# Queries and keys of the last four mLSTM heads as a thirteenth block of the seven-product stage

## The chip, the core and the metric

The kernel runs on one core of one Trainium2 chip. The core has five engines that run side by side, each through its own list of instructions and in order: TensorE (PE in the profile) multiplies matrices into PSUM, VectorE (DVE) and ScalarE (ACT) work element by element, GpSimd (POOL) does the rest of the elementwise work, and SyncE (SP) issues most of the transfers. ACT and POOL issue transfers too. All transfers share sixteen DMA engines. The metric is the device time of one execution in microseconds (us).

## The reference

One decoder layer over 512 tokens of width 2048, in float32. A normalised input is projected by one wide matrix, two token mixers run on parts of the projection, and their outputs are projected back, gated and added.

```
u    = rmsnorm(x, norm_w);  proj = u @ w_in          # 512 x 2048 by 2048 x 20528
ml_q, ml_k (8 heads x 128 each), ml_v, ml_o, ml_z (2048 each), ml_i, ml_f (8 each),
dn_qkv (3 x 2048), dn_z (2048), dn_b, dn_a (16 each), gate_a, gate_b (2048 each) = split(proj)

h_a = mlstm_chunkwise(q * 128**-0.5, k, v, softcap(ml_i + b_i), logsigmoid(softcap(ml_f + b_f)))
h_a = rmsnorm_per_head(h_a) * ml_norm_w * sigmoid(ml_o) * silu(ml_z)
q, k, v = silu(causal_conv4(dn_qkv));  q, k = l2norm(q), l2norm(k)
h_b = gated_delta_chunkwise(q, k, v, sigmoid(dn_b), -exp(a_log) * softplus(dn_a + dt_bias))
h_b = rmsnorm_per_head(h_b, dn_norm_w) * silu(dn_z)
h   = x + sigmoid(gate_a) * (h_a @ w_out[:2048]) + sigmoid(gate_b) * (h_b @ w_out[2048:])
out = rmsnorm(h, final_norm_w)
```

Here only `ml_q` and `ml_k` of heads 4 to 7 matter: 512 columns of `w_in` each, so a product of 512 x 2048 by 2048 x 1024. The mLSTM needs them channel-major (128 channels of a head by 512 tokens, `kq`), and the keys token-major too (`kw`).

## The kernel before

**Products.** Each float32 operand is split into a rounded high part and the rest (`split_hi` on ACT, L135, and `split_lo` on DVE, L138), and each product is three matmuls: high by high, high by low, low by high.

**Two ways to project.** `proj_cm` (L250) gives 256 columns channel-major: two PSUM tiles of 128 channels by 512 tokens, with the weights as the stationary operand; 96 matmuls on lines L261 to L263. `seven` (L565, within `seven_stage`) gives a block of twice 512 columns, `c1` and `c2`, token-major, by a Strassen-like scheme: seven products in place of eight, over 16 sets of weights a block (8 of group A with four products, 8 of group B with three), each product six matmuls on L578 to L580. Sums and differences of weights are made on DVE (L531, L532, L538); one of them goes to DRAM (`t_d`) in group A and is read back in group B. The weights are prepared one set ahead of the products. A "sink" for each kind of block takes the four results: two row tiles come straight from PSUM when a product ends (`end1`, `end5`), two more lie in the SBUF tiles U1 and C22 (`end7`) until the next block writes these. `sink_s` (L697, the DN_Z gates) does for each of eight tiles a copy, a tanh, one vector operation (L704) and a store.

**The order of the work.** PE's instructions run in the order in which the program writes them. The other work is written as generators that a scheduler of the kernel's own advances: `start(gen, wait)` puts one in, and `tick()` advances all that are due. `proj_cm` ticks 16 times in a projection (once for six matmuls), `seven` once for each product (six matmuls too). The other engines' instructions are ordered by a list scheduler with priorities; `urgent` raises one, `behind(e)` holds an instruction until after the newest split or weight load of that engine.

**The stages.** (1) Norms, u, and four projections (`QK`, L145) with queries and keys of heads 0 to 3, stored to `qk_d`. (2) Twelve `seven` blocks (`SEVEN`, L49): four z, two s, two v, four g. (3) The mixers: eight units (`dn_unit`, L1058; `UNITS`, L47), each with projections of K, V and Q of two delta heads (three times 16 ticks). In units 3 to 6 a projection of kind "m" between K and V gives queries and keys of mLSTM head 4, 5, 6 or 7 (128 columns of each), which ACT copies from PSUM to `mkq` (L1076, L1078). (4) The output: two plain blocks, in which unit 7's mixers end, then one more plain block, two seven-product blocks and a last plain one. A tile pool of three PSUM banks, `psw`, serves all small products of the mixers.

**The mixers' chains.** After a unit's projections `dn_back` (L946) starts 25 ticks later, or 9 where the unit had an "m" projection; 11 ticks after that two chains, `dn_chain` (L999), go over four token blocks, handing small products from PE to DVE and ACT and back. `ml_head` (L1099) takes one mLSTM head: it turns the keys token-major (`turn`, L807: a transpose on DVE in 32 x 32 blocks, then `travel`, L814: four stores of 64 KB to DRAM and a load), makes the decay weights, then goes over four token blocks with `pnum` (L1142, L1144) and `pcs`. Heads 0 to 3 come in through `ml_first` (L1184), which loads `kq` from `qk_d`; they start 40 ticks apart. Heads 4 to 7 start behind their own projection. The buffers `mkq`, `mkw` and `mv1` exist once.

```
for h in range(2 * QKFIRST):
    start(ml_first(h), 1 + 40 * h, "B")
for unit in UNITS:
    dn_unit(*unit)
```

Of the kernel before, what the change touches and what calls it, by code (L numbers as in the profile page):

```python
# [15 lines left out]
P = 128  # L16
# [39 lines left out]
def hybrid_body(  # L56
# [83 lines left out]
    def behind(eng):  # L140

        return tc.issue_after(newest[eng])
# [5 lines left out]
    for p, h in UNITS:  # L148
        for kind, c in (("i", DN_K + p * NB), ("m", h), ("i", DN_V + p * NB), ("i", DN_Q + p * NB)):
            if c is not None:  # L150
                plan += [(kind, c, k) for k in range(0, KT, KP)]
# [7 lines left out]

    def load_raw():  # L160
        kind, c, k = plan[len(raws)]
        if kind == "m":

            qk = w_in[k * P:(k + KP) * P, ML_Q:ML_V].rearrange("(k p) (a n) -> p k a n", p=P, a=2)[:, :, :, c * P:(c + 1) * P]
            src, nk, n = None, KP, NB
        elif kind == "i":
            src, nk, n = w_in[k * P:(k + KP) * P, c:c + NB], KP, NB
        else:
            src, nk, n = w_out[k * P:(k + 1) * P, c:c + NO], 1, NO
        with tc.high_priority(offset=2 * PRIO if len(raws) > RAHEAD else 0):  # L170
            raw = wp.tile([P, nk, n], F32, tag="wr", name="wr", bufs=NRAW)
            if src is None:
                for i in range(KP):
                    nc.sync.dma_start(raw[:, i, :].rearrange("p (a n) -> p a n", a=2), qk[:, i])
            else:
                newest["S"] = nc.sync.dma_start(raw, src.rearrange("(k p) n -> p k n", p=P)).ins
        raws.append((raw, nk, n))

    def split_next():
# [67 lines left out]

    JB, WB, OB = (psj, "pj"), (psw, "wk"), (pso, "o")

    def proj_cm(col0, before=None, kind="i"):  # L250
        ps = [psj.tile([P, S], F32, tag="pj", name="pj") for _ in range(2)]
        for kt0 in range(0, KT, KP):
            hi, lo = next_w(kind, col0, kt0)
            if before is not None:
                for k in range(KP):
                    before(kt0 + k)
            for j in range(2):
                for k in range(KP):
                    kt = kt0 + k
                    wsl = slice(j * P, (j + 1) * P)  # L260
                    T.matmul(ps[j], hi[:, k, wsl], uh[:, kt, :], start=(kt == 0), stop=False)  # L261
                    T.matmul(ps[j], hi[:, k, wsl], ul[:, kt, :], start=False, stop=False)  # L262
# [368 lines left out]
    def sink_flat(dst, func, scale):  # L631

        def sink(c1, c2, m1, m5, m7, last):
            def out_(ps, c, col):
                o = spare(last)
                with urgent(3):
                    A.activation(o, ps, func, scale=scale)
                nc.scalar.dma_start(dst(c, col), o)

            def late(x_, c, col):  # L640
                with behind("A"):
                    if func != AF.Copy:
# [12 lines left out]

            return (lambda t: out_(m1[t], t, c1)), end5, end7
        return sink
# [39 lines left out]
    def sink_s(c1, c2, m1, m5, m7, last):  # L697
# [21 lines left out]
        def end7(t):  # L719
# [3 lines left out]

        return (lambda t: out_(m1[t], t, c1, 4)), end5, end7

    SINK = {"g": sink_flat(lambda c, col: tg_d[c, :, col - GATE:col - GATE + NO], AF.Tanh, 0.5),
            "v": sink_flat(lambda c, col: v_d[c, :, col - ML_V:col - ML_V + NO], AF.Copy, 1.0),
            "z": sink_z, "s": sink_s}

# [269 lines left out]
    def dn_chain(j, hs, kq, u):  # L999
# [53 lines left out]
        yield 2  # L1053
        with urgent():
            V.tensor_tensor(out=g, in0=po, in1=g, op=ALU.mult)
        turn(g, h_d[h], True, 5 if h < 2 * UNITS[-1][0] else 3)

    def dn_unit(p, mh):  # L1058
        hs = (2 * p, 2 * p + 1)
        dcol = p * NB  # L1060
        even, last = p % 2 == 0, p == UNITS[-1][0]
        by, front = "B" if even else "A", "B" if even or last else "A"
        u = {"aq": [], "qt": [], "ke": [], "vs": [], "dm": [], "pool": wkb if even else wk}
        kq = [u["pool"].tile([P, 2, S], F32, tag="kq", name=f"kq{h}", bufs=2) for h in hs]
# [4 lines left out]
            conv_silu(ps[j], 16 + hs[j], kq[j][:, 0, :])  # L1069
            start(silu_end(kq[j][:, 0, :], (kq[j][:, 0, :], ke)), 4 + 3 * j, front)  # L1070
        start(dn_front_k(hs, kq, u), 1, front)
        if mh is not None:
            ps = proj_cm(mh, kind="m")
            mkq = wkb.tile([P, 2, S], F32, tag="mkq", name="mkq", bufs=1)
            with urgent():
                A.mul(mkq[:, 1, :], ps[0], float(P) ** -0.5)  # L1076
            with urgent():
                A.copy(mkq[:, 0, :], ps[1])  # L1078
            start(ml_head(mh, mkq), 1, "B")
        ps = proj_cm(DN_V + dcol)  # L1080
        for j in range(2):
            vt = u["pool"].tile([P, NC, P], F32, tag="vn", name="vt", bufs=2)
# [11 lines left out]
            u["qn"].append(qn)  # L1094
            start(silu_end(kq[j][:, 1, :], (kq[j][:, 1, :], qn)), 4 + 3 * j, front)
        start(dn_front_q(hs, kq, u), QWAIT + 3 * last, by)
        start(dn_back(hs, kq, u), (25 if mh is None else 9) + 4 * last, by)

    def ml_head(h, kq):  # L1099
        kT, qT = kq[:, 0, :], kq[:, 1, :]  # L1100
        kw = wkb.tile([P, NC, P], F32, tag="mkw", name="kw", bufs=1)
        with behind("V"):
            turn(kT, kw)
        rb = row_bcast(h, "nrb")
        iwb = wp.tile([P, NC, P], F32, tag="tg", name="iwb", bufs=3)
        G.dma_start(iwb.rearrange("p c t -> p (c t)"), rows_d[8 + h, :].partition_broadcast(P))
# [74 lines left out]
            turn(g[i], hm_d[2 * h + i], True)  # L1181
            yield 4

    def ml_first(h):  # L1184

        kq = wkb.tile([P, 2, S], F32, tag="mkq", name="mkq", bufs=1)
        for i in range(2):
            nc.sync.dma_start(kq[:, 1 - i, :], qk_d[2 * QKFIRST * i + h])
        yield 4
        yield from ml_head(h, kq)  # L1190

    y_d = dr.tile([NC, P, D], F32, tag="yd", name="y_d")

    def open_y():
# [37 lines left out]
            if i > 3:  # L1232
                yield 1

    for h in range(2 * QKFIRST):
        start(ml_first(h), 1 + 40 * h, "B")
    start(open_y(), 200)
    for unit in UNITS:
        dn_unit(*unit)

    h1s, h2s = ctx.enter_context(ExitStack()), ctx.enter_context(ExitStack())
    late = {}
# [446 lines left out]
```

## Time and profile before

| | |
|---|---|
| median of 3 runs | 2215.1 us (2213.11 to 2217.27) |
| profiled execution | 2216.45 us, its span 2214.7 us |
| mean granted TensorE clock | 0.995 |
| PE busy | 97% |
| DVE, ACT, POOL busy | 75%, 46%, 13% |

An "L" number is a line of the kernel. In a row of a group the columns are line, engine, operation, output and inputs, shapes and count, then busy time, mean of one, idle time before. In a row of one line or tile they are the shortest, median and longest duration in ns and the first and last start. In a row of waits: who waited for whom, total us, how often, the longest. In a row of DMA issues: output and input, queue, count, size and the median time from issue to landing. Matmuls overlap, so their durations exceed the step from one to the next.

### The profile page before, as it was taken

What the parts mean: (1) busy time and instruction counts of PE and PEld (TensorE: products, weight loads), DVE (VectorE), ACT (ScalarE), POOL (GpSimd) and SP (SyncE); (2) the same over time, 40 slices, a digit from 0 to 9 for tenths busy, and PEclk for the clock granted to TensorE, in tenths of its full rate; (3) what the DMA queues carried; (4) which work ended last, traced back from release to release, by engine and by line L of the source; (5) the groups of instructions that cost most, each with busy time, mean ns of one, the idle gap of its engine ahead of it and who ended that gap; (6) DMA issues with size and microseconds to landing.
All of it is one profiled execution on the core that took longest, in us unless ns stands there. A gap on an engine that the chain in (4) does not pass through costs nothing. (4 is left out here: it accounts for less than half of the span.)

```text
span 2214.7 us, 31661 instructions
## 1 busy us (share of the span) xinstructions
PE 2153.5 (97%) x10592; PEld 1767.6 (80%) x10592; DVE 1664.4 (75%) x2891; ACT 1024.1 (46%) x1986; POOL 290.7 (13%) x395
## 2 busy tenths in 40 slices
PE   6999999999999999999999999999999999989998
PEld 5877878878888878878888887878888887867776
DVE  5787788788878777777588876757685877577777
ACT  5444444445444444443545644444444454344345
POOL 0320000000000000000223314222222211010100
PEclk9999999999999999999999999999999999999999
DMA  5455666667667766776677767677757668696896
GB/s 157 119 182 188 199 211 195 214 190 239 198 214 233 230 184 224 235 220 219 186 191 177 181 157 179 144 172 171 183 141 173 152 160 231 175 263 187 244 301 215
DMA packets 531174, 433.72 MB, mean 196 GB/s; under 512 B 241857, under 2 KB 393634, under 8 KB 530882
## 3 DMA queue, kind: packets, MB, share of 16 engines
q1 hardware_dynamic: 418738, 345.09, 55.0%
q10 hardware_dynamic: 105568, 68.77, 9.8%
q0 software_dynamic: 6704, 17.83, 3.8%
q8 instruction: 83, 1.36, 0.3%
q14 instruction: 81, 0.66, 0.1%
HBM read 342.37 MB, written 93.39 MB: 197 GB/s over the span
## 5 line engine op out<-in xcount | busy, mean ns | idle before, releaser
L135 ACT CAST wh<-wr 128x512 fp32r<-128x512 f32 (+1 forms) x538 | 379.5, 707 | 417.8 <-PE pj L262 230.3
L138 DVE TENSOR_TENSOR wl<-wr,wh 128x512 fp32r<-128x512 f32 (+1 forms) x538 | 443.0, 826 | 148.0 <-ACT wh L135 134.8
L261 PE MATMUL pj<-uh,wh 128*128 128x512 f32 x1024 | 426.5, 416 | 0.0
L263 PE MATMUL pj<-uh,wl 128*128 128x512 f32 x1024 | 400.9, 391 | 0.0
L262 PE MATMUL pj<-ul,wh 128*128 128x512 f32 x1024 | 400.4, 391 | 0.0
L579 PE MATMUL ps<-wl,uh 128*128 128x512 f32 x704 | 278.1, 395 | 8.1 <-DVE wl L138 7.8
L578 PE MATMUL ps<-wh,uh 128*128 128x512 f32 x704 | 275.7, 392 | 6.5 <-DVE X L626 4.0
L580 PE MATMUL ps<-wh,ul 128*128 128x512 f32 x704 | 274.4, 390 | 0.0
L135 ACT CAST wh<-ts 128x512 fp32r<-128x512 f32 x224 | 138.3, 617 | 262.4 <-DVE ts L538 201.2
L135 ACT CAST wh<-t 128x1024 fp32r<-128x1024 f32 x112 | 117.9, 1053 | 250.1 <-PE ps L580 125.3
L263 PEld LDWEIGHTS pj<-uh,wl 128*128 128x128 f32 x1024 | 192.4, 188 | 42.4
L579 PE MATMUL ps<-wl,suh 128*128 128x512 f32 x576 | 224.2, 389 | 1.6 <-DVE wl L138 1.6
L578 PE MATMUL ps<-wh,suh 128*128 128x512 f32 x576 | 224.7, 390 | 0.9 <-ACT qk L353 0.5
L580 PE MATMUL ps<-wh,sul 128*128 128x512 f32 x576 | 224.1, 389 | 0.0
L261 PEld LDWEIGHTS pj<-uh,wh 128*128 128x128 f32 x1024 | 193.2, 189 | 35.0
L262 PEld LDWEIGHTS pj<-ul,wh 128*128 128x128 f32 x1024 | 193.4, 189 | 32.9
L138 DVE TENSOR_TENSOR wl<-ts,wh 128x512 fp32r<-128x512 f32 x224 | 153.4, 688 | 35.2 <-ACT wh L135 35.2
L138 DVE TENSOR_TENSOR wl<-t,wh 128x1024 fp32r<-128x1024 f32 x112 | 137.0, 1224 | 51.0 <-ACT wh L135 50.5
L579 PEld LDWEIGHTS ps<-wl,uh 128*128 128x128 f32 x704 | 132.1, 188 | 47.7 <-DVE wl L138 21.9
L578 PEld LDWEIGHTS ps<-wh,uh 128*128 128x128 f32 x704 | 132.1, 188 | 40.0 <-DVE X L626 9.6
L538 DVE TENSOR_TENSOR ts<-wr 128x512 f32<-128x512 f32 x112 | 77.2, 689 | 101.0 <-DMA wr<-t_d 80.1
L580 PEld LDWEIGHTS ps<-wh,ul 128*128 128x128 f32 x704 | 132.2, 188 | 26.2
(313 smaller groups left out, 3513.9 us busy)
## 6 DMA issues: line engine op xcount, KB each, us to landing
wr<-in_w_in_dram SPq DMA_DIRECT2D x704, 256.0 KB, 3.7
wr<-in_w_out_dram SPq DMA_DIRECT2D x138, 256.0 KB, 4.7
t_d<-ts ACTq DMA_DIRECT2D x96, 256.0 KB, 4.1
wr<-t_d SPq DMA_DIRECT2D x96, 256.0 KB, 4.0
wr<-in_w_in_dram SPq DMA_DIRECT2D x64, 128.0 KB, 3.2
xt<-in_x_dram SPq DMA_DIRECT2D x8, 512.0 KB, 7.6
tg_d<-X ACTq DMA_DIRECT2D x16, 256.0 KB, 5.5
tg_d<-to ACTq DMA_DIRECT2D x16, 256.0 KB, 5.1
```

What stands on the lines that cost most here:

```text
L135: newest["A"] = A.copy(hi, src).ins
L138: newest["V"] = V.tensor_tensor(out=lo, in0=src, in1=hi.bitcast(F32), op=ALU.subtract).ins
L261: T.matmul(ps[j], hi[:, k, wsl], uh[:, kt, :], start=(kt == 0), stop=False)
L262: T.matmul(ps[j], hi[:, k, wsl], ul[:, kt, :], start=False, stop=False)
L263: T.matmul(ps[j], lo[:, k, wsl], uh[:, kt, :], start=False, stop=(kt == KT - 1))
L538: V.tensor_tensor(out=ts[:, 0, :], in0=r[:, 0, :], in1=r[:, 2, :], op=ALU.subtract)
L578: T.matmul(ps[t], ah, hi, start=(g == "A" and i == 0), stop=False, skip_group_check=True)
L579: T.matmul(ps[t], ah, lo, start=False, stop=False, skip_group_check=True)
L580: T.matmul(ps[t], al, hi, start=False, stop=(i == KH - 1), skip_group_check=True)
```

## The change

`UNITS` loses its second part: no unit has an "m" projection any more, and each lasts 48 ticks. `SEVEN` gains a block "q" between s and v, whose `c1` is the queries and `c2` the keys of heads 4 to 7 (`QKS` is 512). Its `sink_q` scales the queries by 128 ** -0.5, stores the keys token-major to `k_d` and turns all eight tiles of 128 tokens by 512 columns: one transpose on DVE and four stores of 64 KB on ACT's queue into `qt_d`, which holds the heads channel-major. `ml_first` goes into `ml_head`: every head loads `kq` from DRAM, heads 0 to 3 from `qk_d` and 4 to 7 from `qt_d`. Heads 0 to 3 still turn their keys; heads 4 to 7 load `kw` from `k_d`. All eight heads start 42 ticks apart, and `dn_back` starts 25 ticks after each unit (29 after the last, as before).

```
-UNITS = [(p, p + 1 if 2 * QKFIRST - 2 < p < 7 else None) for p in range(8)]
+UNITS = list(range(8))
+QKS = 2 * QKFIRST * P
          + [("s", DN_Z + c, DN_Z + c + NO) for c in range(0, D, 2 * NO)]
+         + [("q", ML_Q + QKS, ML_K + QKS)]
          + [("v", ML_V + c, ML_V + c + NO) for c in range(0, D, 2 * NO)]
...
+    qt_d = dr.tile([4 * QKFIRST, P, S], F32, tag="qtd", name="qt_d")
+    k_d = dr.tile([NC, P, QKS], F32, tag="kd", name="k_d")
...
+    def sink_q(c1, c2, m1, m5, m7, last):
+
+        def turned(x_, c, a):
+            if a:
+                with behind("A"):
+                    nc.scalar.dma_start(k_d[c], x_)
+            o = spare(True)
+            with behind("V"):
+                V.transpose(o, x_)
+            to = qt_d[a * 4:(a + 1) * 4].rearrange("h (j r) (n a c) -> r (h j) n a c", r=BS, n=NC, c=BS)
+            ov = o.rearrange("p (m c) -> p m c", c=BS)
+            for b in range(4):
+                yield 1
+                with behind("A"):
+                    nc.scalar.dma_start(to[:, :, c, b, :], ov[b * BS:(b + 1) * BS])
+
+        def out_(ps, t, a, wait):
+            z = spare(False)
+            with urgent(3):
+                A.mul(z, ps, (float(P) ** -0.5, 1.0)[a])
+            start(turned(z, t, a), wait + 6 * t)
+
+        def end5(t):
+            add(m5[t], U1[t], m5[t])
+            out_(m5[t], t, 1, 8)
+
+        def late_q(t):
+            with behind("A"):
+                A.mul(U1[t], U1[t], float(P) ** -0.5)
+            yield from turned(U1[t], 2 + t, 0)
+
+        def end7(t):
+            add(U1[t], U1[t], m7[t])
+            start(turned(C22[t], 2 + t, 1), 14 + 6 * t)
+            start(late_q(t), 17 + 6 * t)
+
+        return (lambda t: out_(m1[t], t, 0, 4)), end5, end7
...
-        if mh is not None:
-            ps = proj_cm(mh, kind="m")
-            mkq = wkb.tile([P, 2, S], F32, tag="mkq", name="mkq", bufs=1)
-            with urgent():
-                A.mul(mkq[:, 1, :], ps[0], float(P) ** -0.5)
-            with urgent():
-                A.copy(mkq[:, 0, :], ps[1])
-            start(ml_head(mh, mkq), 1, "B")
...
-        start(dn_back(hs, kq, u), (25 if mh is None else 9) + 4 * last, by)
+        start(dn_back(hs, kq, u), 25 + 4 * last, by)
 
-    def ml_head(h, kq):
+    def ml_head(h):
+        kq = wkb.tile([P, 2, S], F32, tag="mkq", name="mkq", bufs=1)
+        kw = wkb.tile([P, NC, P], F32, tag="mkw", name="kw", bufs=1)
+        first = h < 2 * QKFIRST
+        for i in range(2):
+            nc.sync.dma_start(kq[:, 1 - i, :], (qk_d if first else qt_d)[2 * QKFIRST * i + h % (2 * QKFIRST)])
+        yield 4
         kT, qT = kq[:, 0, :], kq[:, 1, :]
-        kw = wkb.tile([P, NC, P], F32, tag="mkw", name="kw", bufs=1)
-        with behind("V"):
-            turn(kT, kw)
+        if first:
+            with behind("V"):
+                turn(kT, kw)
+        else:
+            with behind("S"):
+                nc.sync.dma_start(kw, k_d[:, :, h * P - QKS:(h + 1) * P - QKS].rearrange("c p n -> p c n"))
...
-    for h in range(2 * QKFIRST):
-        start(ml_first(h), 1 + 40 * h, "B")
+    for h in range(MLH):
+        start(ml_head(h), 1 + 42 * h, "B")
```

More of the change, by code (lines that the diff above doesn't have):

```diff
@@ L147, in hybrid_body @@
     nfront = len(plan)
[L148 to L151, printed above, removed]
+    for p in UNITS:
+        for c in (DN_K, DN_V, DN_Q):
+            plan += [("i", c + p * NB, k) for k in range(0, KT, KP)]
     plan += [("o", nb * NO, k) for nb in range(D // NO - 1) for k in range(KT)]
@@ L161, in load_raw @@
         kind, c, k = plan[len(raws)]
[L162 to L166, printed above, removed]
+        if kind == "i":
             src, nk, n = w_in[k * P:(k + KP) * P, c:c + NB], KP, NB
@@ L171, in load_raw @@
             raw = wp.tile([P, nk, n], F32, tag="wr", name="wr", bufs=NRAW)
[L172 to L176, printed above, removed]
+            newest["S"] = nc.sync.dma_start(raw, src.rearrange("(k p) n -> p k n", p=P)).ins
         raws.append((raw, nk, n))
@@ L248, in hybrid_body, with proj_cm @@
     JB, WB, OB = (psj, "pj"), (psw, "wk"), (pso, "o")
-    def proj_cm(col0, before=None, kind="i"):
+    def proj_cm(col0, before=None):
         ps = [psj.tile([P, S], F32, tag="pj", name="pj") for _ in range(2)]
         for kt0 in range(0, KT, KP):
-            hi, lo = next_w(kind, col0, kt0)
+            hi, lo = next_w("i", col0, kt0)
             if before is not None:
@@ L1055, in dn_chain, with dn_unit @@
             V.tensor_tensor(out=g, in0=po, in1=g, op=ALU.mult)
-        turn(g, h_d[h], True, 5 if h < 2 * UNITS[-1][0] else 3)
-    def dn_unit(p, mh):
+        turn(g, h_d[h], True, 5 if h < 2 * UNITS[-1] else 3)
+    def dn_unit(p):
         hs = (2 * p, 2 * p + 1)
         dcol = p * NB
-        even, last = p % 2 == 0, p == UNITS[-1][0]
+        even, last = p % 2 == 0, p == UNITS[-1]
         by, front = "B" if even else "A", "B" if even or last else "A"
@@ L1182, in ml_head @@
             yield 4
[L1184 to L1190, printed above, removed]
     y_d = dr.tile([NC, P, D], F32, tag="yd", name="y_d")
@@ L1233, in load_h @@
                 yield 1
-    for h in range(2 * QKFIRST):
-        start(ml_first(h), 1 + 40 * h, "B")
+    for h in range(MLH):
+        start(ml_head(h), 1 + 42 * h, "B")
     start(open_y(), 200)
     for unit in UNITS:
-        dn_unit(*unit)
+        dn_unit(unit)
     h1s, h2s = ctx.enter_context(ExitStack()), ctx.enter_context(ExitStack())
```

2 lines of the change are left out of this document (1 added, 1 removed).

## The prediction

> **What bounds the kernel now.** I read the engine table first, then the busy times by stage, then what TensorE waited for inside each stage. The stage borders are where the matmul stream changes its line.
>
> ```profile
> span 2214.7 us, 31661 instructions
> PE 2153.5 (97%) x10592; PEld 1767.6 (80%) x10592; DVE 1664.4 (75%) x2891; ACT 1024.1 (46%) x1986; POOL 290.7 (13%) x395
> L261 PE MATMUL pj<-uh,wh 128*128 128x512 f32 x1024 | 426.5, 416 | 0.0
> ...
> 206.80:1063.00 856.20, 848.72 (x3697) 690.13 (x3696) 678.28 (x858) 387.34 (x560) 1.44 (x9) 1.00 0.68 212
> 1063.00:1838.20 775.20, 769.21 (x4418) 643.49 (x4417) 564.39 (x1373) 386.48 (x1004) 213.16 (x288) 1.00 0.71 171
> ```
>
> The last two rows are stretches: borders and length, then busy time (and count) of PE, PEld, DVE, ACT and POOL, the granted clock, the DMA share and GB/s. The first holds blocks 2 to 12 of the seven-product stage, the second the 28 projections of the mixer stage. PE is idle for 7.5 us of 856.2 in the one and for 6.0 us of 775.2 in the other; DVE is busy 79% and 73%. Both stages are set by the number of matmuls that PE issues. A matmul's "mean ns of one" (416) is not its price, since matmuls overlap; the price is the step between starts:
>
> ```profile
> 1063.02 0.39 PE L261 MATMUL pj<-uh,wh 128*128 128x512 f32 x1
> ...
> 1076.85 0.39 PE L262 MATMUL pj<-ul,wh 128*128 128x512 f32 x1
> ```
>
> These are the first and the 62nd of an unbroken run at the start of the first K projection: 13.83 us over 61 steps, 0.2267 us each.
>
> **The change, part by part.**
>
> Removed: four projections of kind "m" (heads 4 to 7). The row above has L261 x1024 for 32 projections, so 32 matmuls on each of three lines, 96 in all. 96 x 0.2267 = 21.8 us each, **-87.1 us** of PE time in the mixer stage, all of it on the path, as PE has no idle time there to speak of.
>
> Added: a thirteenth block of the seven-product stage, 56 products of 6 matmuls = 336 where the four projections had 384. The eleven blocks of the first stretch last 856.2 / 11 = 77.8 us, their waits included: **+77.8 us**. Net -9.3 us. That is all of the gain: one matmul in eight of a 512 x 1024 projection.
>
> The new block's own load beside PE. Its preparation (sums, splits, the round trip of the stored sum) is every block's and is in the 77.8. Its sink does eight tiles: eight PSUM or SBUF tiles scaled or copied on ACT, eight 128x512 transposes on DVE, four plain stores and 32 stores of 64 KB on ACT's queue. The nearest sink is that of DN_Z, which does eight vector operations of the same size:
>
> ```profile
> 518.70:596.20 77.50, 77.00 (x337) 62.81 (x337) 63.92 (x83) 36.86 (x55) 0.00 (x0) 1.00 0.72 222
> L704 DVE SCALAR_TENSOR_TENSOR to<-to x8: 680/682/686, 517.3 to 604.5; 128x512 f32<-128x512 f32 x8
> L811 DVE STREAM_TRANSPOSE to<-vt x16: 691/704/712, 1118.2 to 1825.6; 128x512 f32<-128x512 f32 x16
> L821 ACTq DMA_DIRECT2D hm_d<-to x64: 309/310/1627, 1132.8 to 1786.3; - x64
> ```
>
> A transpose (0.704 us) costs DVE what that sink's operation (0.682 us) costs, so DVE stays at 63.9 of 77.5 us with PE idle for half a microsecond. ACT issues 36 DMAs in place of 8: 28 more x 0.31 = 8.7 us, on top of 36.9 of 77.5. What is queued behind them on ACT is the rounding of the next weights (L135), then DVE's subtraction (L138), then PE; a store that waits for its transpose holds all three. These run one set of weights ahead of PE, 3 to 4 products or 4.1 to 5.4 us (six matmuls are 1.36 us), and the four stores of a tile come one product apart. I take 0 for it; the bounds are -0.7 (no wait in it at all, 7.5 us over 11 blocks) and +3.4, the eight tiles at the mean wait of such a block, 4.4 us in 11:
>
> ```profile
> PE ps L579 <- DVE wl L138: 4.4, 11, 0.9
> ```
>
> That is 0.4 us per wait, 3.2 for eight, and I round it up. Were the cover of one set gone, each tile would show its 0.7 us.
>
> The 32 stores have 512 pieces of 128 bytes each, 16384 packets. Their like is in the mixer stage, 64 of them for hm_d alone:
>
> ```profile
> q10 hardware_dynamic: 105568, 68.77, 9.8%
> t_d<-ts ACTq DMA_DIRECT2D x96, 256.0 KB, 4.1
> hm_d<-to ACTq DMA_DIRECT2D x64, 64.0 KB, 3.6
> ```
>
> One lands in 3.6 us, a whole 256 KB store in 4.1. The queue's packets took 9.8% of 2214.7 us for 105568, 2.06 ns each of all sixteen engines; that mean holds the 2 KB packets too, so 16384 x 2.06 = 34 us is a ceiling. By bytes (2 MB of 68.77) it is 6.6 us, a floor. They spread over some 30 products (42 us), when the weights take a share of about 0.7. I take the lower half, because a 64 KB store lands no later than a large one; then the rings hold and nothing waits. The Trainium skill, "DMA: Bandwidth & Descriptors", Specifications, asks for at least 512 bytes per transfer and says that below it the engine reads, modifies and writes. Here the landing times do not show that penalty; with it the ceiling would hold, which is rival three.
>
> Mixer stage, the work that stays. SP loses 64 loads of 128 KB; for heads 4 to 7 it also loses the turn of k (20 DMAs) and gains three loads each, 12. DVE loses 32 subtractions and four transposes, ACT 32 roundings and eight copies out of PSUM:
>
> ```profile
> L138 DVE TENSOR_TENSOR wl<-wr,wh x538: 641/689/2655, 19.3 to 2180.1; 128x512 fp32r<-128x512 f32 x142, 128x1024 fp32r<-128x1024 f32 x38
> L1076 ACT ACTIVATE mkq<-pj x4: 597/598/600, 1367.2 to 1701.8; 128x512 f32<-128x512 f32 x4
> L1188 SPq DMA_DIRECT2D mkq<-qk_d x8: 326/423/1001, 1029.2 to 1257.3; - x8
> ```
>
> DVE: 564.4 - 32 x 0.689 - 4 x 0.70 = 539.5 us in 775.2 - 87.1 = 688.1, 78%: as dense as the seven-product stage, where PE hardly waits. The kq load of a head stands on SP ahead of weight loads and needs the previous head's mkq free, some 37 ticks after its start; heads were 40 ticks apart and are now 42, and no issue of that load lasted over 1.0 us. I take nothing for it.
>
> What gets denser can be seen in units that had no "m" block. Units 1, 2 (three projections), 3, 4, 5, 6 (four) and 7 (three):
>
> ```profile
> 1135.50:1220.00 84.50, 84.50 (x512) 70.76 (x510) 71.35 (x176) 44.19 (x111) 25.14 (x37) 1.00 0.78 188
> 1220.00:1308.20 88.20, 87.47 (x533) 73.09 (x532) 68.08 (x178) 47.76 (x131) 27.16 (x39) 1.00 0.76 180
> 1308.20:1427.00 118.80, 116.02 (x670) 96.87 (x670) 87.59 (x227) 56.59 (x162) 33.99 (x49) 1.00 0.64 148
> 1427.00:1538.40 111.40, 108.93 (x626) 90.91 (x625) 76.30 (x186) 52.98 (x139) 27.08 (x36) 1.00 0.75 177
> 1647.00:1755.50 108.50, 108.50 (x625) 90.92 (x624) 75.74 (x186) 51.75 (x136) 28.89 (x40) 1.00 0.65 155
> 1755.50:1838.20 82.70, 82.70 (x507) 69.38 (x506) 61.90 (x130) 45.23 (x117) 22.28 (x23) 1.00 0.69 174
> ```
>
> Unit 1 has DVE at 84% and PE idle for nothing; unit 2 waits 0.7 us. The dense shape is not what makes PE wait; the waits of 2.8 and 2.5 us stand in units 3 and 4. But one thing is new. Before, heads 4 to 7 had their C-chain at ticks 52 to 68 of a unit and the delta chains at 20 to 40. With a head every 42 ticks and a back half 25 ticks after each unit, the chain of head 5 (ticks 234 to 250) falls on the delta chains of unit 3 (228 to 248), head 6 on unit 4, head 7 on unit 5. Three streams then hand PSUM banks of one pool of three to DVE and ACT. Their waits in the mixer stage now:
>
> ```profile
> PE p L993 <- ACT s L989: 2.5, 1, 2.5
> PE pk L860 <- DVE kq L795: 2.2, 1, 2.2
> PE pw L1021 <- DVE r L1016: 1.1, 2, 0.7
> ```
>
> A hand-over waits 0.5 us in the mean of L1021. I take one for each of the four heads, **+2 us**; the bounds are -6.0 (every wait of the stage gone) and five units at unit 3's 2.8, less the 5.3 of units 3 and 4, +8.7.
>
> The end of the mixers: unit 6's delta chains shift 16 ticks towards the first output block, where one bank of their pool is taken. Unit 7's chains run there already, and that stretch (1838 to 1998 us) waits for these:
>
> ```profile
> PE py L1330 <- DVE gz L1055: 5.3, 1, 5.3
> PE py L1330 <- ACT wh L135: 2.5, 1, 2.5
> PE py L1330 <- ACT yp L779: 1.7, 2, 1.3
> PE py L1331 <- DVE wl L138: 0.7, 1, 0.7
> ```
>
> The longest is for the last gate (L1055), which unit 7 sets in both kernels; none is for a bank of that pool. The front of unit 7 ends about 22 ticks after its last projection, unit 6's chains now about 20, so buffers are given back no later. 0, with the same bounds as above.
>
> **The sum.** The profiled execution took 2216.45 us (span 2214.7), 1.35 above the median of 2215.1. 2216.45 - 87.1 + 77.8 + 2 = 2209.2; taken from the median, 2207.8. I say **2208**. From no change a measurement of this kernel tells about 0.2%, 4.4 us.
>
> **The rivals.**
>
> One: the waits grow to the bound of +8.7 and take the gain. 2215.1 - 9.3 + 8.7 = 2214.5. For it: units 3 and 4 did wait. Against: units 1 and 2.
>
> Two, the other side: the three streams on one pool open a wait of 2.5 us at each of the four heads, and the clock halves after it. The clock shows this after the last gate:
>
> ```profile
> 1945.00:1955.00 10.00, 7.31 (x24) 5.92 (x25) 7.30 (x13) 2.18 (x3) 0.88 (x1) 0.67 0.80 176
> 1974.00:1999.00 25.00, 21.81 (x84) 17.14 (x83) 18.39 (x27) 11.31 (x19) 4.87 (x7) 0.86 1.01 344
> ```
>
> 0.33 of 10 us is 3.3 us lost after the 5.3 us wait, and 0.14 of 25, 3.5 us, about one of 2.5 us. So 4 x (2.5 + 3.4) = 23.6, 2215.1 - 9.3 + 23.6 = 2229. It decides from 2.3 us per head on. Against it: unit 4's wait of 2.5 us left the clock at 1.00. The Trainium skill, "TensorE: Matmul & The Clock Gate", Part 1, has the clock halved after an idle window of about 3.4 us; by that rule waits of 2.5 us would cost only themselves, some 2216. The second row shows a halved clock with the shorter wait, so I keep the higher price.
>
> Three: the small stores take the ceiling of 34 us of the rings. 0.7 x 77.8 + 34 = 88 us of transfers in 77.8: the weights come 10 us late, 2216.
>
> Four: better than said. No wait in the new block and half of the mixers' 6.0 us gone: 2215.1 - 9.3 - 0.7 - 3.0 = 2202; with all gone 2199.
>
> **How the numbers follow.** My forecast 0.47 (2203.5 to 2211), rival one 0.19, three 0.05, two 0.16, four 0.13. The range leaves out most of rival two and the tail of four: 2199 to 2219; the forecast's own is 2203.5 to 2211. Faster by over 0.2% means under 2210.7: the forecast less a little and rival four, 0.58. Within: the rest of it, one and three, 0.26. Slower: rival two, 0.16.
>
> **What the profile after would show.** L261 to L263 x896 in place of 1024; t_d stores x104; the mixer stage near 690 us with DVE near 78%, thirteen blocks of about 77.8 us, the one behind the new block included. Wrong, if the block after it is over 81 us with waits for L138 (ACT held, or the rings), if units 3 to 7 last over 89 us each with waits at the C-chain or L1021, or if the granted clock falls below 1.00 within the mixers.

## The result and the profile after

Over 22 runs each, the changed kernel takes 2217.5 us and the kernel before 2213.1: a ratio of 1.002 (95% interval 1.0011 to 1.0029), slower by 4.3 us where 7 us less was forecast. Executions of one kernel spread over 12 to 14 us. The profiled execution of before lay 3.3 us above the median of its kernel (2216.45 us), that of after at its median (2217.26), so the two traces differ by 0.8 us only; the other 3.5 us can't be placed in them.

The same views as before: the engine table, the group of the first projection line, and stretches of the seven-product stage from its first block to its last and of the mixers' units 0 to 6 (columns as in the prediction).

```profile
span 2215.5 us, 31630 instructions
PE 2146.3 (97%) x10544; PEld 1762.6 (80%) x10544; DVE 1695.5 (77%) x2937; ACT 1035.8 (47%) x1994; POOL 293.8 (13%) x395
L256 PE MATMUL pj<-uh,wh 128*128 128x512 f32 x896 | 374.1, 417 | 0.7 <-ACT yp L812 0.7
...
125.60:1141.70 1016.10, 1003.85 (x4370) 817.51 (x4369) 806.92 (x1017) 457.80 (x659) 8.15 (x17) 1.00 0.68 212
1141.70:1748.80 607.10, 598.45 (x3504) 500.87 (x3502) 462.51 (x1183) 314.10 (x830) 191.66 (x257) 0.99 0.74 181
```

The saving is there. L256 (L261 before) went from x1024 to x896, and PE has 48 matmuls less, 10.9 us at the step of 0.2267. But PE's busy time fell by only 7.2 us (2153.5 to 2146.3), since part of the work ran at a halved clock, and its idle time grew from 61.2 to 69.2 us. The growth has four places. For three of them these are PE's waits: in the block behind the new one (672 to 754 us), in units 0 to 6 with most of unit 7 (1142 to 1829), and from unit 7 to the start of the output (1749 to 1850):

```profile
PE ps L574 <- DVE wl L142: 3.2, 2, 3.1
...
PE pk L893 <- DVE kq L828: 7.8, 4, 5.3
PE pj L256 <- ACT yp L812: 0.7, 1, 0.7
...
PE pst L1061 <- ACT w L1057: 1.5, 2, 1.1
PE pr L1046 <- DVE st L1067: 1.3, 1, 1.3
PE pw L1054 <- DVE r L1049: 0.4, 1, 0.4
```

The fourth is the output from 1850 to 2000 us, where PE is idle for 10.8 us in place of 8.5. The wait for the rounding of weights there (L1356 for L139) is 3.7 us in this trace and 5.3 us in a second one of the same kernel; no run was made for it, and it stays open.

And these are stretches: the block behind the new one, twelve microseconds in it, the block after that, then units 4 and 5 and twenty microseconds of unit 5.

```profile
672.00:754.10 82.10, 78.74 (x338) 64.01 (x337) 64.67 (x84) 33.27 (x47) 0.00 (x0) 0.98 0.78 215
700.00:712.00 12.00, 8.99 (x32) 7.29 (x33) 7.96 (x11) 4.49 (x7) 0.00 (x0) 0.86 0.95 256
754.10:830.20 76.10, 76.10 (x337) 63.05 (x336) 59.52 (x74) 32.74 (x46) 0.00 (x0) 1.00 0.70 219
...
1472.90:1562.40 89.50, 88.51 (x540) 74.34 (x538) 68.89 (x179) 47.05 (x131) 27.25 (x37) 1.00 0.74 181
1562.40:1660.10 97.70, 91.67 (x541) 76.88 (x540) 70.26 (x179) 47.75 (x130) 29.10 (x39) 0.97 0.69 169
1605.00:1625.00 20.00, 14.69 (x146) 12.05 (x145) 14.30 (x40) 11.27 (x31) 7.72 (x11) 0.83 0.89 214
```

A wait of 3.1 us for L142 and the halved clock behind it (0.14 of 12 us, 1.7 us lost) make that block 82.1 us where its neighbours take 76 to 78. A wait of 5.3 us for the keys of unit 5's second head, and again a halved clock (0.17 of 20, 3.4 us), make unit 5 97.7 us where unit 4 takes 89.5. The timeline of the first place shows how it comes about (ACT, then DVE; start, duration, line; in brackets the idle time before and what ended it):

```profile
691.56 3.78 ACTq L735 DMA_DIRECT2D qt_d<-to  x4
695.46 1.05 ACT L139 CAST wh<-t 128x1024 fp32r<-128x1024 f32 x1 [4.05 <-DMA qt_d<-to]
...
695.61 0.71 DVE L729 STREAM_TRANSPOSE to<-X 128x512 f32<-128x512 f32 x1 [1.36 <-DMA t_d<-ts]
...
701.67 0.71 DVE L729 STREAM_TRANSPOSE to<-X 128x512 f32<-128x512 f32 x1 [1.73 <-DMA t_d<-ts]
702.30 0.65 DVE L142 TENSOR_TENSOR wl<-ts,wh 128x512 fp32r<-128x512 f32 x1
```

ACT stood 4.05 us with four stores of turned data to issue, the rounding of the next weights behind them; DVE stood 1.4 and 1.7 us in front of a transpose, because its output shares three buffers with the sums of weights, whose store was still running; and the subtraction that PE waited for stood behind that transpose.

The second place, unit 5 (DVE, then PE):

```profile
1606.68 0.69 DVE L1214 TENSOR_TENSOR mg<-v,mg 128x512 f32<-128x512 f32 x1
...
1607.97 0.70 DVE L844 STREAM_TRANSPOSE to<-mg 128x512 f32<-128x512 f32 x1
...
1611.08 0.68 DVE L1157 TENSOR_TENSOR wm<-psc,wm 128x512 f32<-128x512 f32 x1
1611.68 0.68 DVE L828 SCALAR_TENSOR_TENSOR kq<-th,kq 128x512 f32<-128x512 f32 x1
...
1612.51 2.04 PE L893 MATMUL pk<-kq 128*128 128x128 f32 x8 [5.31 <-DVE kq L828]
```

Ahead of the keys (L828) DVE has the end of head 5, which is its output gates and their transposes (`mg`, L1214 and L844), and the first product of head 6 (`wm`, L1157).

### The profile page after: what moved, and what is told of

Read it like the earlier page. It is cut to its first block, busy times and chain, and to the rows that moved or that the text cites. A ratio compares the mean times of both kernels' runs of the same rounds, so it can differ in the third digit from the quotient of the medians.

```text
span 2215.5 us, 31630 instructions
## 1 busy us (share of the span) xinstructions
PE 2146.3 (97%) x10544; PEld 1762.6 (80%) x10544; DVE 1695.5 (77%) x2937; ACT 1035.8 (47%) x1994; POOL 293.8 (13%) x395
## 3 DMA queue, kind: packets, MB, share of 16 engines
q10 hardware_dynamic: 124192, 74.02, 10.8%
## 5 line engine op out<-in xcount | busy, mean ns | idle before, releaser
L139 ACT CAST wh<-wr 128x512 fp32r<-128x512 f32 (+1 forms) x522 | 373.2, 717 | 390.4 <-PE pj L257 193.0
L142 DVE TENSOR_TENSOR wl<-wr,wh 128x512 fp32r<-128x512 f32 (+1 forms) x522 | 438.7, 843 | 141.3 <-ACT wh L139 131.6
L256 PE MATMUL pj<-uh,wh 128*128 128x512 f32 x896 | 374.1, 417 | 0.7 <-ACT yp L812 0.7
L258 PE MATMUL pj<-uh,wl 128*128 128x512 f32 x896 | 351.8, 393 | 0.0
L257 PE MATMUL pj<-ul,wh 128*128 128x512 f32 x896 | 351.2, 392 | 0.0
L573 PE MATMUL ps<-wh,uh 128*128 128x512 f32 x752 | 294.9, 392 | 5.3 <-DVE X L621 2.8
L575 PE MATMUL ps<-wh,ul 128*128 128x512 f32 x752 | 293.2, 390 | 0.0
L139 ACT CAST wh<-ts 128x512 fp32r<-128x512 f32 x240 | 148.2, 617 | 275.5 <-DVE ts L533 205.5
L139 ACT CAST wh<-t 128x1024 fp32r<-128x1024 f32 x120 | 126.3, 1053 | 272.9 <-PE ps L575 148.0
L574 PE MATMUL ps<-wl,suh 128*128 128x512 f32 x624 | 243.4, 390 | 4.7 <-DVE wl L142 4.7
L575 PE MATMUL ps<-wh,sul 128*128 128x512 f32 x624 | 243.3, 390 | 0.0
L258 PEld LDWEIGHTS pj<-uh,wl 128*128 128x128 f32 x896 | 169.0, 189 | 37.3
L256 PEld LDWEIGHTS pj<-uh,wh 128*128 128x128 f32 x896 | 169.9, 190 | 31.2 <-ACT yp L812 1.1
L142 DVE TENSOR_TENSOR wl<-ts,wh 128x512 fp32r<-128x512 f32 x240 | 164.4, 688 | 37.5 <-ACT wh L139 37.5
L257 PEld LDWEIGHTS pj<-ul,wh 128*128 128x128 f32 x896 | 169.9, 190 | 28.2
L142 DVE TENSOR_TENSOR wl<-t,wh 128x1024 fp32r<-128x1024 f32 x120 | 147.4, 1228 | 56.6 <-ACT wh L139 56.1
```

Source lines behind the costliest of these rows:

```text
L139: newest["A"] = A.copy(hi, src).ins
L142: newest["V"] = V.tensor_tensor(out=lo, in0=src, in1=hi.bitcast(F32), op=ALU.subtract).ins
L573: T.matmul(ps[t], ah, hi, start=(g == "A" and i == 0), stop=False, skip_group_check=True)
L574: T.matmul(ps[t], ah, lo, start=False, stop=False, skip_group_check=True)
L575: T.matmul(ps[t], al, hi, start=False, stop=(i == KH - 1), skip_group_check=True)
```

## The experiments

Theories at the start: ACT is held by the small stores; the rings are crowded by 128-byte packets; the heads' ends fall on the units' fronts (phase); units of three projections have too little PE time for their other work (density). Each ratio is to runs of the kernel before that were made together with it.

**The control.**

> The changed kernel unchanged, a second profile and five more rounds, as the control for the others. If the two new waits of PE belong to the kernel (any theory that names a place), the wait of about 3 us in the block behind the new one (for L142) and the wait of about 5 us for the normalised keys of unit 5 (L893 for L828) are there again, each within half a microsecond, and the ratio to the kernel before is about 1.002. If they are the luck of one execution, they are under 1 us here or stand elsewhere.

1.0020 (1.0006 to 1.0034). Both waits are there again, 3.2 and 5.2 us, with 9.4 us in all for L893. They belong to the kernel.

**The heads' phase.** Two runs move the starts and nothing else.

```
-        start(ml_head(h), 1 + 42 * h, "B")
+        start(ml_head(h), 1 + 46 * h, "B")                                      # e3
+        start(ml_head(h), 1 + 42 * h if h < 4 else 166 + 48 * (h - 4), "B")     # e4
```

> The mLSTM heads start 46 ticks apart in place of 42, so that the end of heads 4 to 7 (output gates, two transposes, eight stores on ACT) falls at ticks 29 to 35 of a unit, behind the key products of the unit's front (tick 24, 25) and no longer at 7 to 27. Theory phase: the 5.3 us wait and its two or three small companions (7.8 us in all for L893) come from that meeting; they fall below 2 us in all, the half-clock window goes, and the kernel gains 6 to 9 us (ratio 0.998 to 0.999). Theory density: a unit of three projections simply has too little PE time for its vector work; the waits move but stay at 6 us or more in all, and the time stays within 3 us of the changed kernel's.

> Heads 4 to 7 start at ticks 166, 214, 262 and 310, so that the end of each falls at ticks 16 to 24 of units 4 to 7, as that of head 5 does by chance in the changed kernel (13 to 21 of unit 5). Theory phase: each of the units 4 to 7 then shows waits of 3 to 6 us for the normalised keys (L893 for L828), 12 us or more in all, with half-clock windows behind them, and the kernel is 5 to 15 us slower than the changed one. Theory density: the sum of these waits stays near 8 us and the time within 3 us.

46 apart: 2203.8 us, 0.9960 (0.9946 to 0.9974), against the control's 2216.3 us 12.5 us less. Forced meeting: 2223.9 us, 1.0054 (1.0037 to 1.0072), 7.6 us more than the control. With 46 no wait for L893 is left, and the stretch of units 0 to 6 holds:

```profile
1137.60:1728.60 591.00, 591.00 (x3484) 495.20 (x3482) 472.53 (x1168) 309.10 (x814) 184.48 (x254) 1.00 0.75 185
```

PE is never idle in 591.0 us, where the changed kernel took 607.1 and was idle for 8.7 of them; the clock is 1.00 in place of 0.99, and DVE is busier (80% in place of 76%). 20 matmuls of the heads moved behind the stretch, at most 4.5 us at the step of 0.2267. So a unit of three projections is not too short for its other work: the density theory falls. With the forced meeting, by contrast:

```profile
PE pk L893 <- DVE kq L828: 14.1, 7, 4.0
...
1524.00:1545.00 21.00, 18.62 (x166) 14.80 (x166) 14.34 (x40) 13.26 (x36) 8.07 (x11) 0.92 1.00 244
1618.00:1640.00 22.00, 18.02 (x162) 14.52 (x157) 12.01 (x37) 12.29 (x32) 7.09 (x7) 0.84 0.79 182
1708.00:1730.00 22.00, 17.50 (x161) 13.90 (x160) 15.73 (x40) 13.53 (x41) 10.24 (x12) 0.92 0.97 227
```

Units 4, 5 and 6 each have their waits and their halved clock. Unit 7 shows 0.6 us, less than expected. The heads are further apart here (48) than in the changed kernel (42): what decides is where a head falls, not how often one comes. Both runs move a head as a whole; that it is its end that matters is read from the ticks and from DVE's list above.

**What holds the keys there.** At 42, the stores of the heads' outputs go to SP in place of ACT (e8), or the tanh and last multiplication of the keys get a higher priority (e7).

```
-                with behind("A"):
-                    nc.scalar.dma_start(d[:, :, a, :].rearrange("m r c -> r m c"), ov[a * BS:(a + 1) * BS])
+                with behind("S"):                                               # e8
+                    nc.sync.dma_start(d[:, :, a, :].rearrange("m r c -> r m c"), ov[a * BS:(a + 1) * BS])
...
-        with behind("A"):
+        with urgent() if soon else behind("A"):                                 # e7, soon = True for K
             A.activation(th, dst, AF.Tanh)
-        V.scalar_tensor_tensor(out=dst, in0=th, scalar=1.0, in1=dst, op0=ALU.add, op1=ALU.mult)
+        with urgent() if soon else ExitStack():
+            V.scalar_tensor_tensor(out=dst, in0=th, scalar=1.0, in1=dst, op0=ALU.add, op1=ALU.mult)
```

> On the changed kernel, heads 42 ticks apart: the stores of the heads' turned outputs (h_d, hm_d, L854), 128 of 64 KB, are issued by SP in place of ACT. Theory ACT in the mixers: the 5.2 us wait of unit 5 came because ACT stood in these stores, which wait for DVE's transposes, with the tanh of the keys behind them; it falls below 2 us, the waits for L893 below 3 us in all (9.4 before), and the kernel gains 5 us or more. Theory DVE: DVE's own list (gates, two transposes, the convolution) is too long at that place whatever ACT does; the wait stays at 4 to 6 us. SP may pay: its weight loads stand behind stores that wait, shown as waits of ACT for w_in.

> On the changed kernel, heads 42 ticks apart: the tanh and the last multiplication of a unit's keys (L827, L828 for K) get a raised priority and are no longer held behind ACT's newest rounding; nothing else moves. If the 5.2 us wait of unit 5 is a matter of order (the tanh stood behind a head's decay weights and stores that could have waited), the waits for L893 fall from 9.4 to under 3 us in all and the kernel gains 5 us or more over the changed one. If DVE and ACT have too much to do at that place in whatever order, the wait moves to the convolution, the roundings (L257) or the chains, their sum stays at 6 us or more, and the time stays within 3 us.

e8: 2214.5 us, 1.0017 (1.0004 to 1.0030). The wait falls from 5.2 to 3.8 us and its companions go, but the time does not move by what can be told; ACT now stands 2.9 us in front of the tanh for DVE's convolution. e7: 2216.1 us, 1.0016 (1.0005 to 1.0026), and the wait changes its name:

```profile
PE pk L894 <- DVE wm L1158: 5.7, 1, 5.7
PE pk L894 <- DVE kq L829: 2.6, 1, 2.6
```

Now the same products wait 5.7 us for a PSUM bank that DVE has not yet read for an mLSTM head. ACT's stores were about a quarter of it; neither they nor the order alone are the cause. At that place the lists of DVE and ACT hold too much in each of the orders tried, and of these edits only moving the heads away helped. `dn_back`, which since the change starts 16 ticks later after units 3 to 6 and whose last gates (`gz`) DVE does just ahead of these steps, was not moved; what that would do is open.

**The turning: who issues, and when.** The 32 stores go to SP (e2, at 42); or the four stores of a tile go out in one tick (e5, at 46).

```
-                yield 1
-                with behind("A"):
-                    nc.scalar.dma_start(to[:, :, c, b, :], ov[b * BS:(b + 1) * BS])
+                yield 1
+                with behind("S"):                                               # e2
+                    nc.sync.dma_start(to[:, :, c, b, :], ov[b * BS:(b + 1) * BS])
...
+            yield 1                                                             # e5: one yield ahead of the four
```

> The 32 stores of 64 KB of the new block's sink are issued by SP in place of ACT, nothing else is changed. Theory ACT: ACT stood in the issue of these stores (four took 3.8 us) with the rounding of the next weights behind them; then the 3.1 us wait for L142 in the block behind falls below 1 us, that block comes down from 82.1 to about 78 us, the half-clock window behind the wait goes, and the kernel gains 3 to 5 us (ratio to before 1.000). Theory rings: the 16384 packets of 128 bytes delay the weights whoever issues them; then the wait stays at 2 to 4 us and the time does not move. A third way: SP is held in its turn, weight loads come late, and waits for DMA appear in front of the sums of weights (L526, L533); then the block is 80 us or more.

> On the version with heads 46 ticks apart: the four stores of a turned tile go out in one tick, one tick behind the transpose, in place of one a tick. The SBUF tile that holds the turned data shares three buffers with the sums of weights; it is then held some 4 us less. Theory buffers: DVE stood for 1 to 2 us in front of a transpose or a sum until one of these buffers came free, and that made the 3.1 us wait for L142 in the block behind the new one; it falls below 1.5 us and the kernel gains 2 to 4 us over the version with 46. Theory ACT: ACT stands while it issues the stores, and four in a row hold the rounding of the weights longer; the wait stays at 3 us or grows to 5. Theory rings: the packets are the same and closer together; the wait stays at 3 us or grows too.

e2: 2216.4 us, 1.0022 (1.0008 to 1.0037); e5: 2206.8 us, 0.9981 (0.9969 to 0.9993), not better than 46 alone (0.9960). In both, the 3.1 us wait is gone and others stand in its place, in the block behind the new one (e2, then e5):

```profile
PE ps L574 <- DVE wl L142: 2.8, 4, 0.8
PE ps L573 <- DVE X L621: 1.4, 3, 0.9
...
PE ps L573 <- DVE X L621: 2.2, 2, 2.0
PE ps L574 <- DVE wl L142: 1.3, 2, 0.7
```

So ACT's standing was one way in which the crowd showed, not the cause by itself. e5 frees the shared buffers sooner, but issues the stores closer together, and gains nothing; a ring of buffers of the sink's own was not tried.

**The turning: left out, or thinned out.** The flat sink stores eight tiles as they are, and heads 4 to 7 are computed from the queries and keys of heads 0 to 3. The spread sink makes the same eight turns over 45 products in place of 31, the tiles in U1 and C22 first.

```
-            start(turned(C22[t], 2 + t, 1), 14 + 6 * t)                         # spread: end7
-            start(late_q(t), 17 + 6 * t)
+            start(turned(C22[t], 2 + t, 1), 2 + 10 * t)
+            start(late_q(t), 7 + 10 * t)
...                                                # out_: wait 38 for 8 (m5), 27 for 4 (m1)
-            o = spare(True)                       # flat: no transpose, no stores to qt_d
+            with behind("A"):
+                nc.scalar.dma_start((k_d if a else q_d)[c], x_)
```

> On the version with heads 46 ticks apart: the new block's sink stores its eight tiles as they are, token-major, with one store each; the eight transposes and the 32 stores of 64 KB are left out, and heads 4 to 7 load the queries and keys of heads 0 to 3 as kq, so the four heads are computed from wrong data. What is left is the price of the block itself. If the turning is what costs (theories ACT, buffers and rings alike), the block behind the new one falls from about 81 to 77 or 78 us, no wait there is over 1 us, and the kernel gains 3 to 5 us over the version with 46. If the wait belongs to the block's preparation, it stays at 3 us.

> On the version with heads 46 ticks apart: the same eight turns of the new block's sink, but over 45 products in place of 31, first the four tiles in U1 and C22 and then the four in their own buffers, one tile in five or six products. Theory crowding (ACT, the shared buffers and the rings are three faces of it): the wait of 3.1 us for L142 falls below 1 us, the block behind comes down from 81 to 78 us, and half or more of the 6.7 us that leaving out the turning gained is got (ratio to before near 0.994). If a single turn already holds the next weights, whatever its distance to the next, the waits are only spread: 3 us in all and no gain.

> The changed kernel, heads 42 apart, with the sink's turns spread over 45 products and nothing else. If the 3.1 us wait and the half clock behind it are the price of the turning, it gains 3 to 5 us over the changed kernel (ratio to before 1.000) and the block behind is 78 us. If not, the wait goes but the time stays at 1.002.

> The changed kernel, heads 42 apart, with the turning left out (plain stores, heads 4 to 7 computed from the queries and keys of heads 0 to 3). It prices the turning at the changed kernel's own spacing: 3 to 5 us if it is the wait and the half clock (ratio 1.000), 6 to 7 us if what was seen at 46 holds here too (ratio 0.999); the waits for L893 in units 4 to 6 stay as they were, since they come from the heads.

| | heads 42 apart | heads 46 apart |
|---|---|---|
| sink as changed | 1.0020 (1.0006 to 1.0034) | 0.9960 (0.9946 to 0.9974) |
| spread | 0.9994 (0.9983 to 1.0006) | 0.9960 (0.9944 to 0.9975) |
| flat | 0.9995 (0.9982 to 1.0007) | 0.9936 (0.9922 to 0.9950) |

At 42 both gain alike, 0.0026 and 0.0025 of 2213 us, 5.8 and 5.5 us, each with some 4 us to either side: the price of the turning in the changed kernel, and spreading it can't be told from leaving it out. The block behind the new one, spread, at 42:

```profile
671.40:749.20 77.80, 76.52 (x337) 62.99 (x336) 64.07 (x84) 32.61 (x47) 0.00 (x0) 1.00 0.83 228
```

The same packets cross the same rings in this block (a share of 0.83, more than the 0.78 above), and PE waits 1.3 us in all. Nor did transfers land late in the crowd. In its stretch of the changed kernel (672 to 715 us) the median store of a sum landed after 4.5 us and the median weight load after 4.2; at 596 to 640 us of the kernel before it was 5.4 and 4.6, and no wait of PE there is over 0.4 us. So the rings are not the cause. At 46 the spread sink alone shows no gain over 46, though its wait is gone there too, and the flat one 5.3 us; the intervals are 3 us to either side and overlap. That difference stays open.

**The chains of unit 6.** They now run beside `load_h`, and in the trace ACT stands in front of tiles on their way from `hm_d`. At 46: one tile in two ticks (e9), or the rounding held behind the newest splits (e10).

```
-                split_scaled(uh[:, k, :], ul[:, k, :], raws_[i][:, n, :], normc[:, 16 + k:17 + k])
-                yield 1
+                split_scaled(uh[:, k, :], ul[:, k, :], raws_[i][:, n, :], normc[:, 16 + k:17 + k])
+                yield 2                                                         # e9, without the later yield 1
...
+                with behind("A"), behind("V"):                                  # e10
+                    split_scaled(uh[:, k, :], ul[:, k, :], raws_[i][:, n, :], normc[:, 16 + k:17 + k])
```

> On the version with heads 46 ticks apart: the rounding of the mLSTM outputs for the output stage (load_h, L1231, L1232) goes one tile in two ticks in place of one in one, so that ACT no longer stands in front of a tile that is still on its way from hm_d (5.7 us there). Theory: unit 6's chains, which now run beside it, are queued behind it on ACT and DVE, and that makes the waits of 1.1, 2.8 and 0.9 us for L1061 and L1054 near 1800 to 1830 us; they fall below 1.5 us in all, and the kernel gains 3 to 5 us. Rival: the chains wait for each other over the pool of PSUM banks, of which the first output block holds one; then the waits stay. Third: the products of the first output block come to need their rounded tile too early and wait for it (L1356 for L1231); then nothing is gained.

> On the version with heads 46 ticks apart: the rounding of the mLSTM outputs (load_h, L1231, L1232) is held behind the newest split of ACT and of DVE, so that the scheduler can't put it earlier in ACT's list. Spreading it over more ticks had left ACT standing 5.1 us in front of a tile on its way. Theory ACT in front of the load: ACT's waits for hr<-hm_d fall below 3 us each, and the waits of PE for L1054 and L1061 near 1800 to 1830 us from 3.8 to 4.8 to under 1.5 us in all; gain 2 to 4 us over 46 alone. Rival, PSUM banks: they stay at 3 us or more. Third: the first output block waits for its tiles (L1356 for L1231).

e9: 2203.2 us, 0.9961 (0.9947 to 0.9975). ACT's longest wait stayed (5.1 us), so the edit did not do what it was made for. e10: 2201.5 us, 0.9951 (0.9937 to 0.9966). PE's waits there, for 46 alone and then for e10:

```profile
PE pw L1054 <- DVE r L1049: 2.8, 1, 2.8
PE pst L1061 <- ACT w L1057: 2.2, 3, 1.1
...
PE pst L1061 <- ACT w L1057: 1.9, 1, 1.9
PE pr L1046 <- DVE st L1067: 1.0, 1, 1.0
PE pw L1054 <- DVE r L1049: 0.6, 2, 0.4
```

5.0 us became 3.5, and 0.0009 of the ratio is inside the intervals, while ACT still waited up to 5.9 us for `hr`. That these waits are new with the change is seen in the traces; that `load_h` causes them is argued, not shown.

**The best version**, 46 apart with the spread sink and e10's edit, and the same with the flat sink (heads 4 to 7 again from the wrong data).

> Heads 46 ticks apart, the sink spread over 45 products, and load_h held behind the splits: the sum of what the two other runs of this call show. By the theories 3 to 5 us from the sink and 2 to 4 us from load_h, so 2195 to 2199 us; if one of the two fails there, that part is missing here too.

> The best version so far (heads 46 apart, sink spread, load_h held back; 2200.3 us) with the turning left out: plain stores only, heads 4 to 7 computed from the queries and keys of heads 0 to 3. If the spread sink already hides the turning, this is within 2 us of that version, 2198 to 2201 us; if the turning costs by its mere work on DVE, ACT and the rings, it is 4 to 7 us faster, 2193 to 2196 us.

2200.3 us, 0.9947 (0.9928 to 0.9966), and flat 2201.0 us, 0.9940 (0.9923 to 0.9958). No difference that can be told, with 4 us to either side: spread, the turning is hidden as far as these runs show. This version beats both kernels, the one before by 0.5%, but can't be told from 46 apart alone (0.9960); its PE is busy 98% of the span.

## Why the prediction was wrong

**The saving** was right: x896, 48 matmuls less, a thirteenth block at the price of the others ((1141.7 - 206.8) / 12 = 77.9 us, the disturbed one included). So were DVE's 78% (76% in units 0 to 6) and the reading that dense units do not make PE wait: with 46 PE is never idle in them. That kernel's 0.9960 (0.9946 to 0.9974) also holds the forecast, 2208 / 2215.1 = 0.9968, but by luck: it has no wait in units 0 to 6, where 2 us more of them were forecast, and it still pays for the turning, which was put at 0.

**"I take 0 for it; the bounds are -0.7 ... and +3.4"** (the new sink) failed: it cost 5.5 to 5.8 us by the medians, and the trace shows 4.8 in the block behind the new one (3.1 waited, 1.7 lost to the halved clock), both beyond the bound of +3.4. The prediction's own sign of it came, a block of over 81 us with a wait for the subtraction of weights. Its work was priced right (DVE 64.7 us in that block, 63.9 forecast), its crowding not: eight turns were taken as eight independent waits of 0.4 us, while they came in 31 products, one after the other through the same three buffers and the same ACT, and added up to one wait long enough to halve the clock. The buffers, which the sums of weights share, were not in the working at all.

**"A hand-over waits 0.5 us ... +2 us"** failed by size and place. I looked for the meeting between a head's chain and the delta chains; those did fall on each other, and in units 0 to 6 no wait of PE for a chain is to be found. The costly meeting was that of a head's end (ticks 42 to 50 after its start) with the unit's front (tick 24). Counted as the prediction counts, from the 6.0 us of waits of before, 46 apart stands for -6.0 and 42 apart for some 12.5 us more, +6.5: inside the bounds, but 4.5 above the +2. Rival two had the right form, a wait of some microseconds with a halved clock behind it, at the wrong place.

The profile of before showed the meeting once, and the prediction shows its row (L860 for L795, 2.2 us) without reading it as one. By the ticks head 3 ends at 163 to 171, which is 19 to 27 of unit 3, and DVE's list there has the same steps of a head's end ahead of the keys. The clock of the stretch stayed at 1.00 (DVE, then PE, then the stretch):

```profile
1352.05 0.68 DVE L1180 TENSOR_TENSOR mg<-v,mg 128x512 f32<-128x512 f32 x1
1352.76 0.71 DVE L811 STREAM_TRANSPOSE to<-mg 128x512 f32<-128x512 f32 x1
...
1354.32 0.69 DVE L795 SCALAR_TENSOR_TENSOR kq<-th,kq 128x512 f32<-128x512 f32 x1
...
1355.07 1.16 PE L860 MATMUL pk<-kq 128*128 128x128 f32 x8 [2.17 <-DVE kq L795]
...
1350.00:1370.00 20.00, 17.83 (x179) 14.29 (x179) 14.34 (x40) 12.73 (x32) 7.83 (x10) 1.00 0.93 208
```

So unit 3's 2.8 us, which the bound of +8.7 was built on, was for the most part this meeting and not a chain's hand-over. The size of 5.3 us and the halved clock behind it could not be seen there; the place could, by the count that I made for the chains, made for every step of a head.

**"0, with the same bounds as above"** (unit 6's chains) was a little low: unit 7's chains run beside the output block, but not beside `load_h`. 3.2 us of waits stand where the kernel before had 1.7 (L1330 for L779), and no run shows what they cost in time.

**The base**: 2215.1 us was the median of three; that of 22 is 2213.1, so 2 us of the forecast's level were off.

**The terms together**, as an estimate from these runs: -9.3 for the matmuls, +6.5 for the heads, +5.6 for the turning and +1.5 at the end of the mixers make +4.3 us, where +4.3 was measured. That it comes out so closely is luck: two of the terms have some 4 us to either side, and the output's 2.3 us are not in it.

## What to carry to other kernels

Taking work from the engine that bounds a kernel can take away the cover that other work had; here the mean load was not what cost time, but which steps met, so count the ticks of every step that is moved, to its last store, against the tight points of its neighbours. Where a repeating task is started at a fixed spacing beside another of a different period, try several spacings: here four ticks were worth 12.5 us, more than the change's whole saving of 9.3. A short wait of the same kind in the old profile is worth placing by the ticks, since it may be the one that grows. Small work should be spread over all the time there is; whether buffers of its own would have helped was not tried.

## What the runs showed of the hardware

The halved clock follows short waits, though not each of them. The wait of 2.5 us in unit 4 of the kernel before and that of 2.2 us in its unit 3 left it at 1.00. It followed the single wait of 3.1 us above, a single one of 2.6 us in e7, and in the control two waits of 1.0 and 1.5 us, less than five microseconds apart (stretches of before, e7 and the control):

```profile
1450.00:1465.00 15.00, 12.54 (x79) 10.34 (x80) 6.50 (x10) 6.74 (x17) 1.21 (x2) 1.00 0.75 190
...
1515.00:1530.00 15.00, 12.42 (x130) 10.16 (x129) 12.47 (x34) 7.36 (x21) 2.48 (x6) 0.89 1.03 250
...
1512.00:1530.00 18.00, 15.49 (x142) 12.30 (x142) 16.29 (x41) 10.52 (x32) 4.25 (x7) 0.91 0.99 227
```

0.09 of 18 us is 1.6 us lost. So the halved clock that the prediction laid to a wait of 2.5 us (1974 to 1999 us) need not be that wait's alone: 0.8 us after it stands another, of 0.7 us. The Trainium skill, "TensorE: Matmul & The Clock Gate", Part 1, has it that an idle window of about 3.4 us halves the clock and that the window runs freely. In these traces shorter waits, down to 2.6 us, were followed by a halved clock, and so were two whose sum is 2.5 us. The halved clock makes a wait half as dear again, or more: 1.7 us behind 3.1 and 3.4 us behind 5.3.
